# A feed-forward's closing products spread over the next unit, and a chunk's two down groups interleaved behind its last unit, with TensorE in program order

## The chip, the core and the metric

The kernel runs on one core of a Trainium2 chip. The metric is the time of one execution on the device in microseconds; several runs are made, and their median is given. The core has a matrix engine (TensorE, PE), a vector engine (VectorE, DVE), a scalar engine (ScalarE, ACT), a general engine (GpSimd, POOL) and an engine that here issues transfers (SyncE, SP). Each engine works through its own list of instructions in order, and an instruction waits for the ones on other engines that it depends on.

## The reference

One step of a decoder layer for 544 tokens (512 of a prompt and 8 requests with 4 tokens each), width 1024, hidden width 2816, in float32:

```python
def swiglu(x, wg, wu, wd):
    return (jax.nn.silu(x @ wg) * (x @ wu)) @ wd

x = layer_norm(ALPHA * x + 0.5 * swiglu(x, ffn1_wg, ffn1_wu, ffn1_wd), ln1_g, ln1_b)
...
x = layer_norm(ALPHA * x + mix, ln2_g, ln2_b)
x = layer_norm(ALPHA * x + 0.5 * swiglu(x, ffn2_wg, ffn2_wu, ffn2_wd), ln3_g, ln3_b)
```

The line left out is the mixing (RWKV-7 heads and a gated short convolution). The change touches only the two feed-forward parts, which are built by the same code. The first one fills the time from about 12 to 345 us, the second from about 700 to 1075 us.

## The kernel before, in words

Tokens lie along the columns, features along the 128 partitions. A float32 product is made of three matmuls in a reduced format: each operand x is split into a high part (an ACT copy) and a low part (DVE subtracts the high part from x), and high x high, high x low and low x high are summed in PSUM. For weights the two halves of a split are L147 (ACT) and L148 (DVE), 1024 columns at a time, into one of a few tiles hl; raw weights arrive in a few tiles raw. For activations they are L151 and L152.

The 22 hidden tiles are worked in chunks of 4, 4, 4, 4 and 6 (chunk 0 to chunk 4). For each chunk its hidden activations are computed from x, and, but for the last chunk, sent through the down weights at once and added to z, the running sum. Both steps use a Strassen-Winograd scheme: a 2 x 2 block product with seven instead of eight block products, for which sums of blocks are made first on DVE and the results are combined on DVE and ACT.

* A **unit** (pairs) is such a scheme for two hidden tiles and either the gate or the up half (even u: gate, with Silu; odd u: up, multiplied in). A product is 12 matmuls of 272 columns. The weights of a unit are split as four parts: x and a as loaded, b (the second half of x), and y, for which DVE adds blocks in two instructions first (L486, L487) and then the split follows. The products of a unit are, in their order: a at 0, a at HK, y at HK, x at HK, x at 0 (below "x0"), b, y. The last two, the **tail**, are written behind the first two products of the next unit. Where a result of PSUM bank b1 is used twice, ACT copies it out in between (L581, L587, L590 into cpb) and the next product adds on in the bank. So product x0 must wait for L587, and product b for L590. The tail's results are combined by L545 to L567 into the rows hk and sv, and put_h (L341 to L350, then L151 and L152) makes the blocks B11, NT1, B21, NT2, T3, T4 and, by put_b22, B22, that the down step multiplies.
* A **down group** (g = 0, 1) does the same for four of the eight output tiles. Its seven steps are p1, p3, p4, p5, p6, p2, p7, each with two half products (q = 0, 1) of 6 matmuls. p1 needs B11, p3 NT1, p4 B21, p5 NT2 and the weights y, p6 T3, p2 T4 and the weights b, p7 B22. DVE adds p1, p4 and p2 to z (L610), ACT copies p5 and p6 out (L626, L629), DVE subtracts p3 (L630) and adds p7 (L636), and POOL issues a DMA that accumulates the copies to the second half of z (L637): z<-cpb for group 0, z<-sv for group 1. The rows sv and the columns of cpb are written again by the next chunk's units, which so wait for these DMAs.
* Chunk 0's hidden tiles come from the plain products of up (L365, L369), and the **last chunk** has no down groups: its activations are split into hhl, and down (L390) sends them through the weights d by d.

When a weight part is split is set by a table that plan makes: for each unit or group with its start t, counted in products, part p is put at t - LEAD[p] (x 7, a 9, y 5, b 18 and other values), and feed, called at each product, issues what is due, loads too. A held instruction (hold) keeps a split from being ordered ahead of it on its engine. The order of the rest is set by a scheduler, which may slide PE's matmuls past each other as long as PSUM and data allow: pinned is False here, so the loops below say only roughly in which order PE works.

## Time and profile before

| | us |
|---|---|
| runs: median (lowest, highest) | 1082.21 (1079.39, 1083.17) |
| the profiled execution, its own time | 1080.19 |
| its span, first to last instruction | 1078.4 |
| PE busy, 8960 matmuls | 1054.3 (98%) |
| DVE busy, 1528 instructions | 833.0 (77%) |
| ACT busy, 1015 instructions | 564.3 (52%) |
| POOL busy | 206.4 (19%) |
| granted PE clock, as a share of full speed | 0.991 |

Busy shares are averages over the whole span. Where an engine works in order, what counts is which wait ends last at a place: a row of the timeline gives an instruction's start, its length, and in brackets how long its engine stood idle before it and on what. PE's matmuls overlap at their ends, so that their pace is read from start to start. The difference between a run's time and its span, 1.8 us here, lies around the first and the last instruction.

### The profile page before, as it was taken

Reading aid. Unit: us, or ns where it says so; the run is one execution under the profiler, and the core shown is the slowest. Engines: PE = TensorE matmul, PEld = TensorE weight load, DVE = VectorE, ACT = ScalarE, POOL = GpSimd, SP = SyncE. Lnnn points to the kernel's source line nnn. Section 1 sums busy time; section 2 is a strip of 40 time slices with the busy share of each in tenths; the row PEclk is TensorE's granted clock in tenths of the full one; section 3 lists DMA queues with packets and bytes.
Section 4 is the critical chain, followed back from the end, with each engine's and each line's share of the span. In section 5 each row is a group of like instructions: output and inputs, shape, how many; then the busy total and the mean of one; then the engine's idle time right before and its main releaser. Section 6 shows DMA issues by size and latency. Waiting matters only on the chain.

```text
span 1078.4 us, 22059 instructions
## 1 busy us (share of the span) xinstructions
PE 1054.3 (98%) x8960; PEld 1021.0 (95%) x8960; DVE 833.0 (77%) x1528; ACT 564.3 (52%) x1015; POOL 206.4 (19%) x296
## 2 busy tenths in 40 slices
PE   9999999999999999999999999999999999999996
PEld 8999999999999998888989899999999999999995
DVE  7798888889775857787588578878889888887755
ACT  6655565555552567555312464466554655545524
POOL 0122230312200023343220410010313122130000
PEclk9999999999999999999989999999999999999998
DMA  8568595866854231222616631424957759496302
GB/s 295 129 125 191 124 216 134 177 158 145 197 122 147 77 116 40 69 52 87 153 59 200 237 104 40 138 59 89 213 145 164 178 125 225 105 211 138 104 1 84
DMA packets 82887, 144.78 MB, mean 134 GB/s; under 512 B 20448, under 2 KB 44384, under 8 KB 82528
## 3 DMA queue, kind: packets, MB, share of 16 engines
q1 hardware_dynamic: 55584, 107.19, 30.7%
q0 software_dynamic: 27200, 36.18, 21.7%
q8 instruction: 70, 1.15, 0.4%
q14 instruction: 33, 0.27, 0.1%
HBM read 124.37 MB, written 10.06 MB: 125 GB/s over the span
## 4 chain that ended last, share of the span: by engine, by line
PE 79%; DVE 9%; DMA 6%; ACT 3%; issue 2%; SPq 0%; POOL 0%; ACTq 0%; DVEq 0%; POOLq 0%
PE mm L76 50%; PE sm L76 29%; DVE hl L148 2%; DMA z<-sv 2%; DMA z<-cpb 1%; ACT hl L147 1%; DVE De L1008 1%; DMA raw<-in_gu 1%; DVE SC L955 1%; DVE tm L1006 1%; DVE hhl L152 1%; DMA raw<-in_wd 1%; DMA DM<-Dd 1%; DMA z<-in_xT 0%; DVE z L610 0%
## 5 line engine op out<-in xcount | busy, mean ns | idle before, releaser
L76 PE MATMUL mm<-xhl,hl 128*128 128x288 f32 (+2 forms) x2640 | 362.8, 293 | 3.5 <-DVE hl L148 2.3
L76 PEld LDWEIGHTS mm<-xhl,hl 128*128 128x128 f32 x2640 | 343.6, 189 | 11.2 <-DVE hl L148 2.5
L148 DVE TENSOR_TENSOR hl<-raw,hl 128x1024 fp32r<-128x1024 f32 (+3 forms) x224 | 262.0, 1175 | 69.1 <-ACT hl L147 68.3
L147 ACT ACTIVATE hl<-raw 128x1024 fp32r<-128x1024 f32 (+3 forms) x224 | 224.4, 1012 | 91.6 <-DVE raw L487 31.3
L76 PE MATMUL sm<-xhl,hl 128*128 128x272 f32 (+1 forms) x1392 | 193.8, 289 | 0.3 <-DVE xhl L152 0.3
L76 PEld LDWEIGHTS sm<-xhl,hl 128*128 128x128 f32 x1392 | 182.3, 189 | 1.5 <-ACT xhl L151 0.6
L76 PE MATMUL mm<-tv,hl 128*128 128x272 f32 x864 | 121.3, 289 | 1.9 <-ACT cpb L587 1.8
L76 PE MATMUL mm<-hhl,hl 128*128 128x272 f32 (+2 forms) x792 | 119.2, 294 | 0.1
L76 PEld LDWEIGHTS mm<-tv,hl 128*128 128x128 f32 x864 | 113.3, 188 | 3.0 <-ACT cpb L587 2.3
L76 PEld LDWEIGHTS mm<-hhl,hl 128*128 128x128 f32 x792 | 105.9, 188 | 5.1 <-ACT sv L626 1.5
L76 PE MATMUL sm<-hhl,hl 128*128 128x272 f32 (+2 forms) x792 | 109.6, 288 | 0.0
L76 PEld LDWEIGHTS sm<-hhl,hl 128*128 128x128 f32 x792 | 103.0, 188 | 0.5
L493 POOL DMA_DIRECT2D raw<-in_gu x36 | 43.5, 1209 | 256.2 <-DVE cpb L583 81.4
L499 POOL DMA_DIRECT2D raw<-in_wd x32 | 39.3, 1469 | 269.2 <-DVE hlb L152 235.6
L76 PE MATMUL mm<-tv,hlb 128*128 128x272 f32 x432 | 61.1, 291 | 0.8 <-ACT cpb L590 0.8
L76 PEld LDWEIGHTS mm<-tv,hlb 128*128 128x128 f32 x432 | 56.4, 188 | 2.3 <-ACT cpb L590 2.2
L151 ACT ACTIVATE hhl<-sv 128x272 fp32r<-128x272 f32 (+1 forms) x52 | 26.0, 512 | 30.8 <-DVE sv L350 12.1
L152 DVE TENSOR_TENSOR hlb<-raw,hlb 128x512 fp32r<-128x512 f32 x52 | 35.7, 687 | 4.2 <-ACT hlb L151 4.2
L151 ACT ACTIVATE hhl<-hk 128x272 fp32r<-128x272 f32 (+1 forms) x48 | 24.2, 504 | 27.5 <-DVE hk L557 12.9
L218 ACT ACTIVATE lnq<-z 128x512 f32<-128x512 f32 (+1 forms) x24 | 14.9, 654 | 41.5 <-DVE z L217 41.5
L487 DVE TENSOR_TENSOR raw<-raw 128x512 f32<-128x512 f32 x52 | 35.8, 689 | 1.0
L76 PE MATMUL mm<-hhl,hlb 128*128 128x272 f32 (+2 forms) x264 | 36.4, 288 | 0.0
(294 smaller groups left out, 1325.9 us busy)
## 6 DMA issues: line engine op xcount, KB each, us to landing
raw<-in_gu SPq DMA_DIRECT2D x84, 512.0 KB, 4.6
raw<-in_gu POOLq DMA_DIRECT2D x36, 512.0 KB, 6.2
raw<-in_wd SPq DMA_DIRECT2D x32, 512.0 KB, 4.7
raw<-in_win SPq DMA_DIRECT2D x26, 512.0 KB, 3.6
raw<-in_wd POOLq DMA_DIRECT2D x32, 256.0 KB, 6.0
raw<-in_wd SPq DMA_DIRECT2D x16, 384.0 KB, 3.1
z<-cpb POOLq DMA_DIRECT2D x16, 272.0 KB, 9.0
z<-sv POOLq DMA_DIRECT2D x16, 272.0 KB, 7.3
```

The costliest lines, as they stand in the source:

```text
L76: ins = f(*args, **kw)
L147: ACT.activation(hl[:, 0, a:b], raw[:, a:b], AF.Copy)
L148: DVE.tensor_tensor(hl[:, 1, a:b], raw[:, a:b], hl[:, 0, a:b].bitcast(F32), op=OP.subtract)
L151: ACT.activation(hi, x, AF.Copy)
L152: DVE.tensor_tensor(lo, x, hi.bitcast(F32), op=OP.subtract)
L218: sq = ACT.activation(qq, zz, AF.Square)
L487: DVE.tensor_tensor(y[:, :, 0], y[:, :, 1], a[:, :, 1], op=OP.add)
L493: POOL.dma_start(x.rearrange("p (s c) -> p s c", s=2), bass.AP(tensor=a11.tensor, offset=a11.offset, ap=[[2 * D, P], [P * 2 * D, 2], [1, 5 ...
L499: POOL.dma_start(four(x)[:, i], bass.AP(tensor=a11.tensor, offset=a11.offset, ap=[[DFF, P], [P * DFF, 2], [1, 256]]), accum_op=OP.add)
L955: DVE.tensor_tensor(SC[:, p, par, a0c:a0c + n, :], q[:, :P * n].rearrange("p (c t) -> p c t", c=n), (msk if n > 1 else msks)[:, None, :].t ...
L1006: DVE.tensor_tensor(tv, AT[:, k, k + 1:32, None].to_broadcast([P, n, k + 1]), De[:, k, None, 0:k + 1].to_broadcast([P, n, k + 1]), op=OP.mult)
L1008: DVE.tensor_tensor(De[:, k + 1:32, 0:k + 1], De[:, k + 1:32, 0:k + 1], tv, op=OP.add)
```

## The change

* The tail is split in two. Product b of a unit still stands behind the next unit's two a products, but product y and what follows it now stands two products later, between x at HK and x0. For this the copy behind x0 (L590, now L602) gets columns of cpb of its own, and odd and even units use other columns.
* The chunk's last unit keeps its tail for downs, which now runs both groups in one sequence: p1 of group 0, the unit's b and y, p3(0), p1(1), p4(0), then the blocks T4 and B22 are made, p5(0), p5(1), p6(0), p3(1), p2(0), p6(1), p7(0), p2(1), p4(1). The last step, p7 of group 1, is handed to the next chunk, which does it behind its first product.
* The table of put times changes with it: group 0 of chunks 1 to 3 is counted from t - 2, group 1 from t + 4, with its y no earlier than t + 2.
* PE is kept in program order from chunk 0's down groups to the last chunk's last unit.

```diff
@@ plan
+                    add((ci, "u", u), t, dict(LEAD, b=LEAD_B.get(u, LEAD["b"] if u == 2 else 15)))
+                    t += 7
+                if ci < LAST:
+                    add((ci, "d", 0), t - 2 if ci else t, LEAD)
+                    add((ci, "d", 1), t + 4, LEAD, y=t + 2)
+                    t += 28
@@ pairs
-            def tail(u, b1, b3, cp):
+            def tail_b(u, b1, b3, cp, c2):
...
+            def tail_y(u, b1, b3, cp, c2):
...
                     if ci < LAST:
-                        self.put_h(j, 0, ("hi", "t4") if j else ("hi",))
-                        if j:
-                            self.put_b22()
+                        self.put_h(j, 0, ("hi",))
...
-                a = 0 if u % 2 else 3 * TB
-                cp = cpb[:, a:a + 3 * TB]
+                a = 0 if u % 2 else 4 * TB
+                cp, c2 = cpb[:, a:a + 2 * TB], cpb[:, (2 if u % 2 else 3) * TB:][:, :TB]
...
                 hold(ACT.activation(cp[:, 0:TB], b1, AF.Copy))
+                if u == 0:
+                    yield from self.tails.pop(0)
                 yield from prod(b4, u, "a", HK, xb(HK, 0), True)
                 hold(DVE.tensor_tensor(cp[:, 0:TB], cp[:, 0:TB], b4, op=OP.add))
-                if old is not None:
-                    yield from old
+                if u:
+                    yield from self.tails.pop(0)
                 yield from prod(b1, u, "y", HK, tb(0), False)
                 hold(ACT.activation(cp[:, TB:2 * TB], b1, AF.Copy))
                 yield from prod(b3, u, "x", HK, xb(0, TB), True)
+                if u:
+                    yield from self.tails.pop(0)
                 yield from prod(b1, u, "x", 0, tb(1), False)
-                hold(ACT.activation(cp[:, 2 * TB:], b1, AF.Copy),
-                     DVE.tensor_tensor(cp[:, 2 * TB:], cp[:, 2 * TB:], b3, op=OP.add))
-                old = tail(u, b1, b3, cp)
-            yield from old
+                hold(ACT.activation(c2, b1, AF.Copy), DVE.tensor_tensor(c2, c2, b3, op=OP.add))
+                self.tails = [tail_b(u, b1, b3, cp, c2), tail_y(u, b1, b3, cp, c2)]
@@ downs
+            yield from step["p1"](0)
+            for x in tails:
+                yield from x
+            yield from step["p3"](0)
+            b1 += [s1(), s0()]
+            yield from step["p1"](1)
+            yield from step["p4"](0)
+            if ci:
+                self.put_h(1, 0, ("t4",))
+                self.put_b22()
+            for p, g in (("p5", 0), ("p5", 1), ("p6", 0)):
+                yield from step[p](g)
+            b3 += [s0(), s0()]
+            for p, g in (("p3", 1), ("p2", 0), ("p6", 1), ("p7", 0), ("p2", 1)):
+                yield from step[p](g)
+            b4 += [s1(), s1()]
+            yield from step["p4"](1)
+            self.rest = step["p7"](1)
@@ main
+            pinned[0] = True
             for ci in range(LAST + 1):
                 if ci:
-                    yield from self.pairs(ci)
+                    yield from self.pairs(ci, self.rest)
                 if ci < LAST:
-                    yield from self.downs(ci)
+                    yield from self.downs(ci, self.tails if ci else [])
+            for x in self.tails:
+                yield from x
+            pinned[0] = False
```

The changed file has other line numbers: L486, L487 become L492, L493; L545, L547, L548 L551, L553, L554; L555 and L557 L561 and L563; L563, L565, L567 L573, L575, L577; L581, L587 L589, L597; L590 and L591 both L602; L610 L618; L626 L639; L629, L630 L628, L629; L636, L637 L632, L633. L76 to L390 are the same.

PE at the first full boundary (chunk 1), with buffer numbers. mm_1283 is b1 of chunk 1's last unit before, mm_1291 after; hlb is a part b; tv and xhl are the unit's inputs, hhl the blocks for the down groups. The rows before run from the product x0 to the first matmul of p5 of group 0:

```order
L76 MATMUL mm_1283<-tv_284,hl_1197 128x272 x12
L76 MATMUL mm_1448<-hhl_88,hl_1286 128x272 x4
L76 MATMUL mm_1283<-tv_284,hlb_1060 128x272 x12
L76 MATMUL sm_1285<-xhl_68,hl_1235 128x272 x12
L76 MATMUL mm_1448<-hhl_88,hl_1286 128x272 x2
L76 MATMUL mm_1449<-hhl_88,hl_1286 128x272 x6
L76 MATMUL sm_1450<-hhl_88,hl_1316 128x272 x6
L76 MATMUL sm_1451<-hhl_88,hl_1316 128x272 x6
L76 MATMUL sm_1452<-hhl_88,hl_1286 128x272 x6
L76 MATMUL sm_1453<-hhl_88,hl_1286 128x272 x6
L76 MATMUL mm_1448<-hhl_88,hl_1346 128x272
L76 MATMUL mm_1577<-hhl_88,hl_1491 128x272 x2
```

and after, from product b to p5 of both groups (its hl_1469 is group 1's part y):

```order
L76 MATMUL mm_1291<-tv_284,hlb_1060 128x272 x12
L76 MATMUL sm_1293<-xhl_68,hl_1236 128x272 x12
L76 MATMUL sm_1409<-hhl_88,hl_1294 128x272 x6
L76 MATMUL sm_1410<-hhl_88,hl_1294 128x272 x6
L76 MATMUL mm_1494<-hhl_88,hl_1359 128x272 x6
L76 MATMUL sm_1495<-hhl_88,hl_1359 128x272 x6
L76 MATMUL sm_1407<-hhl_88,hl_1257 128x272 x6
L76 MATMUL sm_1408<-hhl_88,hl_1257 128x272 x6
L76 MATMUL mm_1405<-hhl_88,hl_1324 128x272 x6
L76 MATMUL mm_1406<-hhl_88,hl_1324 128x272 x6
L76 MATMUL mm_1494<-hhl_88,hl_1469 128x272 x6
L76 MATMUL sm_1495<-hhl_88,hl_1469 128x272 x6
```

Before, four matmuls of p1 stood between x0 and b, and group 1 (mm_1577, with hl_1491) came in by single pairs of matmuls behind p4; after, all of p1 stands there, p1 of group 1 (mm_1494, hl_1359) goes ahead of p4, and p5 of group 1 stands right behind that of group 0.

DVE at the same place, around the two additions for part y of group 1's weights. Before:

```order
L148 TENSOR_TENSOR hl_1508<-raw_1115,hl_1508 128x1024
L630 TENSOR_TENSOR cpb_71<-cpb_71,sm_1450 128x272
L486 TENSOR_TENSOR raw_1115<-raw_1115,raw_1240 128x2x256
L630 TENSOR_TENSOR cpb_71<-cpb_71,sm_1451 128x272
L487 TENSOR_TENSOR raw_1115<-raw_1115,raw_1240 128x2x256
L610 TENSOR_TENSOR z_77<-z_77,mm_1448 128x272
L610 TENSOR_TENSOR z_77<-z_77,mm_1449 128x272
L152 TENSOR_TENSOR hlb_1557<-raw_1353,hlb_1557 128x512
L148 TENSOR_TENSOR hl_1526<-raw_1115,hl_1526 128x1024
```

and after:

```order
L346 SCALAR_TENSOR_TENSOR hk_89<-hk_89,sv_90 128x272
L347 TENSOR_TENSOR hk_89<-sv_90,hk_89 128x272
L492 TENSOR_TENSOR raw_1119<-raw_1119,raw_1241 128x2x256
L152 TENSOR_TENSOR hhl_88<-sv_90,hhl_88 128x272
L152 TENSOR_TENSOR hhl_88<-hk_89,hhl_88 128x2x272
L493 TENSOR_TENSOR raw_1119<-raw_1119,raw_1241 128x2x256
L152 TENSOR_TENSOR hlb_1484<-raw_1243,hlb_1484 128x512
L618 TENSOR_TENSOR z_77<-z_77,mm_1494 128x272
L618 TENSOR_TENSOR z_77<-z_77,sm_1495 128x272
L148 TENSOR_TENSOR hl_1469<-raw_1119,hl_1469 128x1024
```

Before, L486 and L487 stood among the steps of group 0's p6; after, L492 and L493 stand between the instructions that make NT2, T3 and T4 (L346, L347 and L152 on hhl), ahead of p1's additions for group 1.

ACT at the same place, around the copy that product b waits for. Before (L590):

```order
L587 ACTIVATE cpb_71<-mm_1283 128x272
L151 ACTIVATE hlb_1368<-raw_1115 128x512
L147 ACTIVATE hl_1346<-raw_1000 128x1024
L151 ACTIVATE hhl_88<-sv_90 128x272
L590 ACTIVATE cpb_71<-mm_1283 128x272
L151 ACTIVATE hlb_1474<-raw_1242 128x512
```

and after (L602), the same six places:

```order
L597 ACTIVATE cpb_71<-mm_1291 128x272
L147 ACTIVATE hl_1359<-raw_1241 128x1024
L575 ACTIVATE sv_90<-cpb_71 128x544
L147 ACTIVATE hl_1388<-raw_1119 128x1024
L602 ACTIVATE cpb_71<-mm_1291 128x272
L151 ACTIVATE hhl_88<-sv_90 128x272
```

Before, one split of 1024 columns (L147, hl_1346) and two short ones stood between L587's place and L590; after, two splits of group 1's weights (hl_1359 and hl_1388) and L575 stand ahead of L602.

More of the change, by code (lines that the diff above doesn't have):

```diff
@@ L446, in plan, with add @@
             items, t, events = [], 0, []
+            def add(key, at, lead, **least):
+                items.append(key)
+                events.extend((max(at - lead[part], least.get(part, -99)), key, part) for part in LEAD)
             for ci, (m0, m1) in enumerate(CHUNKS):
[L448 to L453 removed]
+                for u in range(m1 - m0 if ci else 0):
+                    add((ci, "u", u), t, dict(LEAD, b=LEAD_B.get(u, LEAD["b"] if u == 2 else 15)))
[4 more added lines that the diff above has]
+                    t += 28
             events.sort(key=lambda e: e[0])
@@ L524, in prod, with pairs @@
                     yield 6 * (TB / 2.4 + 3)
-        def pairs(self, ci):
+        def pairs(self, ci, before):
             m0, m1 = CHUNKS[ci]
@@ L544, in tail @@
                 if i == 0:
-                    hold(ACT.activation(s[:, 1, hi], cp[:, 2 * TB:], AF.Silu, scale=-1.0))
+                    hold(ACT.activation(s[:, 1, hi], c2, AF.Silu, scale=-1.0))
                 else:
-                    DVE.scalar_tensor_tensor(s[:, 1, hi], cp[:, 2 * TB:], -1.0, s[:, 1, hi], op0=OP.mult, op1=OP.mult)
+                    DVE.scalar_tensor_tensor(s[:, 1, hi], c2, -1.0, s[:, 1, hi], op0=OP.mult, op1=OP.mult)
                     hold(DVE.tensor_tensor(s[:, 0, lo], s[:, 0, lo], cp[:, 0:TB], op=OP.mult))
@@ L561, in tail @@
                         split(self.hhl[:, 0, 2 * j + 1], self.hhl[:, 1, 2 * j + 1], s[:, 1])
+            def tail_y(u, b1, b3, cp, c2):
+                j, i = divmod(u, 2)
+                s = self.rows[0] if ci < LAST and j == 0 else sv
                 yield from prod(b3, u, "y", 0, xb(HK, TB), False)
@@ new lines, in downs, with add, prods @@
+            cp = [c.rearrange("p (r t) -> p r t", r=2) for c in cps]
+            s0, s1 = (lambda: sm()[:, :TB]), (lambda: big()[:, :TB])
+            b1, b4, b3 = [s1(), s1()], [s0(), s0()], [s0(), s0()]
+            def add(d, o, op=OP.add):
+                hold(DVE.tensor_tensor(z[:, d, lo], z[:, d, lo], o, op=op))
+            def prods(g, dst, part, s, v, first, use):
+                for q in range(2):
+                    off = 2 * q if part == "b" else 4 * q + 2 * s
+                    yield from self.prod(dst[2 * g + q], (ci, "d", g), part, off, blk(v), first, 2)
+                    i, d = 2 * g + q, 4 * g + 2 * q
+                    use(i, d, dst[i])
@@ new lines, in neg, with last @@
+            def neg(i, d, o):
+                hold(ACT.activation(cp[i][:, 1], o, AF.Copy, scale=-1.0),
+                     DVE.tensor_tensor(cp[i][:, 1], cp[i][:, 1], b3[i], op=OP.subtract))
+            def last(i, d, o):
+                hold(DVE.tensor_tensor(cp[i][:, 0], cp[i][:, 0], o, op=OP.add))
+                POOL.dma_start(z[:, d:d + 2, TB:], cp[i], accum_op=OP.add)
+            step = dict(
+                p1=lambda g: prods(g, b1, "a", 0, B11, True, lambda i, d, o: add(d, o)),
+                p3=lambda g: prods(g, b3, "x", 1, NT1, True, lambda i, d, o: None),
+                p4=lambda g: prods(g, b4, "a", 1, B21, True, lambda i, d, o: add(d, o)),
+                p5=lambda g: prods(g, b1, "y", 1, NT2, False, lambda i, d, o: hold(ACT.activation(cp[i][:, 0], o, AF.Copy))),
+                p6=lambda g: prods(g, b1, "x", 0, T3, False, neg),
+                p2=lambda g: prods(g, b1, "b", 0, T4, False, lambda i, d, o: add(d + 1, o, OP.subtract)),
+                p7=lambda g: prods(g, b3, "y", 0, B22, False, last))
```

41 lines of the change are left out of this document (2 added, 39 removed).

## Prediction

> **What bounds the kernel now.** I read the page first. TensorE (PE) is busy nearly all of the span, so the kernel is its matmuls, whose number the change keeps, plus the gaps between them.
>
> ```profile
> PE 1054.3 (98%) x8960; PEld 1021.0 (95%) x8960; DVE 833.0 (77%) x1528; ACT 564.3 (52%) x1015; POOL 206.4 (19%) x296
> ```
>
> Next the waits of PE and of its weight loads (PEld), as engine, line waited for, total us, times, longest. These rows belong to the feed-forward parts:
>
> ```profile
> PE mm L76 <- ACT cpb L587: 1.8, 2, 1.4
> PE mm L76 <- ACT cpb L590: 0.8, 1, 0.8
> PEld mm L76 <- ACT cpb L590: 2.2, 7, 1.0
> PEld mm L76 <- ACT sv L626: 1.5, 8, 0.2
> PEld mm L76 <- DVE hhl L152: 1.3, 6, 0.2
> PEld mm L76 <- ACT cpb L581: 0.5, 2, 0.3
> ```
>
> Six or eight of each: they sit at the chunk boundaries, where a chunk's last unit meets its down groups (three full boundaries and one behind chunk 0 in each feed-forward part). The windows around the first full boundary and over units alone show it:
>
> ```profile
> 117.00:145.00 28.00, 27.99 (x218) 27.27 (x217) 25.27 (x49) 15.11 (x26) 6.67 (x6) 1.00 0.78 158
> 145.00:181.00 36.00, 36.00 (x288) 35.97 (x287) 29.41 (x47) 19.98 (x35) 7.40 (x7) 1.00 0.71 172
> ```
>
> Inside units 288 matmuls take 36.00 us, 125 ns each, without a gap. At the boundary DVE is busy 25.27 of 28 us (90%) and ACT 15.11, so DVE is the engine that can be late. PE's own rows there, and two behind chunk 0:
>
> ```profile
> 115.96 0.67 PE L76 MATMUL mm<-hhl,hl 128*128 128x272 f32 x4
> 116.61 1.77 PE L76 MATMUL mm<-tv,hlb 128*128 128x272 f32 x12
> 118.22 1.67 PE L76 MATMUL sm<-xhl,hl 128*128 128x272 f32 x12
> ...
> 123.73 3.01 PE L76 MATMUL mm<-hhl,hl 128*128 128x272 f32 x20
> 126.61 0.39 PE L76 MATMUL sm<-hhl,hl 128*128 128x272 f32 x1
> 126.90 1.03 PE L76 MATMUL mm<-hhl,hl 128*128 128x272 f32 x6
> 127.76 1.67 PE L76 MATMUL mm<-hhl,hlb 128*128 128x272 f32 x12
> ```
> ```profile
> 61.80 1.64 PE L76 MATMUL mm<-hhl,hl 128*128 128x272 f32 x10
> 63.27 1.67 PE L76 MATMUL mm<-hhl,hlb 128*128 128x272 f32 x12
> ```
>
> Start to start less 125 ns a matmul is the stall: 0.15 before product b, 0.11 in it (the first matmul after a stall takes about 0.1 longer), 0.38, 0.16 and 0.11 around p5: 0.9. The L626 waits of the second group (up to 0.2 each, with the restart 0.1) bring about 0.3: **1.2 us a boundary**. Behind chunk 0 the first group shows 0.22, the second about 0.3: 0.55. All of this is 6 x 1.2 + 2 x 0.55 = 8.3 us; with the last chunk's stalls below, some 12 us of 1080 is the most the change could win.
>
> **Prices.** Start-to-start times of back-to-back work:
>
> ```profile
> 117.07 0.44 DVE L547 SCALAR_TENSOR_TENSOR sv<-cpb,sv 128x272 f32<-128x272 f32 x1
> 117.54 0.44 DVE L346 SCALAR_TENSOR_TENSOR hk<-hk,sv 128x272 f32<-128x272 f32 x1
> ...
> 123.50 0.72 DVE L152 TENSOR_TENSOR hhl<-hk,hhl 128x544 fp32r<-128x544 f32 x1
> 124.14 0.43 DVE L152 TENSOR_TENSOR hhl<-sv,hhl 128x272 fp32r<-128x272 f32 x1
> 124.49 0.43 DVE L610 TENSOR_TENSOR z<-z,mm 128x272 f32<-128x272 f32 x1
> ...
> 125.79 1.22 DVE L148 TENSOR_TENSOR hl<-raw,hl 128x1024 fp32r<-128x1024 f32 x1
> 126.93 0.43 DVE L610 TENSOR_TENSOR z<-z,sm 128x272 f32<-128x272 f32 x1
> ...
> 128.76 0.69 DVE L486 TENSOR_TENSOR raw<-raw 128x512 f32<-128x512 f32 x1
> 129.36 0.43 DVE L630 TENSOR_TENSOR cpb<-cpb,sm 128x272 f32<-128x272 f32 x1
> ```
> ```profile
> 116.16 0.40 ACT L590 ACTIVATE cpb<-mm 128x272 f32<-128x272 f32 x1 [0.84 <-PE mm L76]
> 125.50 1.06 ACT L147 ACTIVATE hl<-raw 128x1024 fp32r<-128x1024 f32 x1
> 126.45 0.39 ACT L626 ACTIVATE cpb<-mm 128x272 f32<-128x272 f32 x1
> 130.43 2.01 ACT L147 ACTIVATE hl<-raw 128x1024 fp32r<-128x1024 f32 x2 [1.55 <-DVE raw L487]
> ```
>
> So DVE takes 0.35 us for 272 columns (0.47 when the next one needs its result), 0.64 for 544, 0.60 for 512, 1.14 for 1024; ACT 0.95 for a 1024 split. Product x0 ended at 115.96 and L590 began at 116.16: 0.20 from PE to its reader.
>
> The Trainium skill ("VectorE: DVE Perf Modes", section "The DRAIN you can't avoid") says that a DVE operation starts only when the one before has left the pipe. The rows disagree where operations are independent: 0.43 long, 0.35 apart. By that rule each would cost its whole length; what this would do is the last rival below.
>
> **The full boundary, walked through after's order.** Let 0 be the start of the last unit's x0, each product 1.51 us: p1(0) at 1.51, b 3.02, y 4.5, p3(0) 6.0, p1(1) 7.5, p4(0) 9.0, p5(0) 10.55, p5(1) 12.06.
>
> *Product b.* On ACT the copy that frees b's bank (L602) now stands behind a weight split that itself waits for x0's end (1.51 + 0.20): split from 1.7, L602 from 2.67 to 3.07, b due at 3.02. With the restart 0.2, and PE has no other matmuls to slip in, as it had four at 115.96.
>
> *p5(1), the heart of it.* Before, the second group's y weights were needed half a boundary after the first's. Now p5(1) follows p5(0), and y's two DVE additions (L492, L493) stand at the end of 23 DVE instructions that begin 0.2 after y(2)'s end: 17 of 272, two each of 544, 512 and 1024: 5.95 + 1.28 + 1.20 + 2.28 = 10.7 us, plus 0.4 for dependent pairs and 0.75 waiting for the first split from ACT: 0.2 + 11.85 = 12.05. Then ACT's split, 12.1 to 13.2, and DVE's low half (L148), behind a 512 and two 272, 13.35 to 14.6. PE wants the high half at 12.06 plus what it is late by then (0.8): 0.4 more; and the low half at its third matmul, 13.6: 1.0, restart 0.1.
>
> *p5(0).* The low half of its activations (L152 with 544 columns, just before L493) ends at 11.5; wanted at about 11.0: 0.5, restart 0.1.
>
> Sum 0.2 + 0.6 + 0.4 + 1.1 = 2.3 against 1.2: **+1.1 a boundary, +6.6 in six**. The bounds: 1.2 (no change), if DVE enters the boundary a microsecond ahead; 2.9, if each of the first three waits lies in front of the next.
>
> *Chunk 0.*
>
> ```profile
> 55.45 0.45 DVE L369 TENSOR_TENSOR sv<-sv,mm 128x288 f32<-128x288 f32 x1 [0.17 <-PE mm L76]
> ```
>
> This row stands 0.3 after p1(0)'s start. After, a group-1 split (1.14, less about 0.3 of idle time) goes ahead of it: it ends at 1.5 from that start. Until L493 is done come seven of 272 columns, two of 544 and three of 512, 5.5, with dependents 5.8: 7.3. ACT's split ends at 8.3, the low half at 9.5; p5(1) is due at 5 x 1.51 = 7.55, its third matmul at 8.6 by then: 0.75 + 0.9 + 0.1 = 1.75 against 0.55, **+1.2, twice: +2.4** (bounds 0 and 1.6 each).
>
> *Costs nothing:* y moved behind xHK inside units: what waits for it, L573 and L575, has a product more before their columns are reused, and cpb columns are now doubled. POOL's and SP's queues keep their order; only the last two accumulating DMAs of a chunk go a product later, behind unit 0's first product, and are wanted in the next chunk's units.
>
> *Next chunk's unit 0.* Its copy waited for z<-cpb (the L581 row); with other columns that goes: **-0.5**.
>
> *The last chunk.*
>
> ```profile
> 283.51 0.43 ACT L545 ACTIVATE sv<-cpb 128x272 f32<-128x272 f32 x1 [2.45 <-DMA z<-sv]
> 286.53 0.66 ACT L565 ACTIVATE sv<-cpb 128x544 f32<-128x544 f32 x1 [1.35 <-DVE cpb L563]
> 287.53 1.78 PE L76 MATMUL mm<-tv,hl 128*128 128x272 f32 x12 [0.41 <-ACT cpb L587]
> 976.23 1.78 PE L76 MATMUL mm<-tv,hl 128*128 128x272 f32 x12 [1.42 <-ACT cpb L587]
> 1020.57 0.63 ACT L147 ACTIVATE hlb<-raw 128x512 fp32r<-128x512 f32 x1 [2.43 <-DMA raw<-in_wd]
> 1021.10 0.38 ACT L590 ACTIVATE cpb<-mm 128x272 f32<-128x272 f32 x1
> 1021.53 1.78 PE L76 MATMUL mm<-tv,hlb 128*128 128x272 f32 x12 [0.75 <-ACT cpb L590]
> ```
>
> At its start ACT waits for z<-sv, then its copy L587 stood behind L565, which waited 1.35 for y. After, L597 stands ahead of that, and is wanted a product (1.5) later; z<-sv also goes a product later. The 1.35 and L565's half microsecond are won: all of the first stall (0.67), some 0.6 of the second: **-1.3** (bounds 0 and -2.3). At the second part's end a split that waits for a weight load stands ahead of L602 still; PE loses the four matmuls that covered 0.5, and L597 ahead of two splits delays that load 0.3: **+0.9** (bounds 0, 1.4).
>
> Sum: 6.6 + 2.4 - 0.5 - 1.3 + 0.9 = **+8.1**. The profiled execution took 1080.19 us (span 1078.4), so 1088.3. Its runs were 1079.39 to 1083.17, median 1082.21; that the profiled one lies 2.0 under the median stays in the range.
>
> **Rivals.**
> *DVE keeps ahead (faster).* If DVE works off the first third of the boundary while y(2) still runs, L493 ends 1.6 us earlier, by 10.5, and every y half is there in time; that is the point where it turns. For it: in the boundary window DVE still has 2.7 us of idle time. Against: those come later, and the 23 instructions cannot start before y(2) and L573. A boundary then costs 0.3 (restarts): -0.9 x 6 - 0.25 x 2 - 0.5 - 1.3 + 0.9 = -6.8, 1073.4; half of it 1077.
> *The waits only change places.* y arrives a microsecond earlier than walked, and p5(1) waits as long as the three old places did: 1.2 again; the rest cancels: 1080, within 0.3%.
> *A fixed PE order waits inside units.* Each of the 18 + 18 units loses 0.3 where the scheduler slipped matmuls in: +11 more, 1099. Against it: no unit shows a gap now, and their order is nearly the old one.
> *DVE operations don't overlap.* 23 x 0.08 = 1.8 us more ahead of L493 at eight places: +14, 1102; the 0.35 spacings speak against it. This is what the rule of the Trainium skill named above would give.
>
> **How the numbers follow.** A measurement of this kernel can tell about 0.3% (3 us) from no change. Chances: forecast 0.45, DVE ahead 0.30, places changed 0.18, units 0.05, no overlap 0.02. So faster 0.30, same 0.18, slower 0.52. The forecast's own range is 1083 to 1093: boundaries at +0.3 each below, at their upper bounds (+1.7, chunk 0 +1.6) above. The whole range, 1075 to 1093, reaches half into the faster case and leaves out its lower part (0.12) and the last two (0.07).
>
> **What would show it.** Right: PE idle under two names at every boundary, the waits of p5(1)'s weights (DVE hl L148, ACT hl L147) near 1.4 together and DVE hhl L152 near 0.5; the boundary's DVE idle gone; L587's stall at 287 gone. Wrong: no wait of mm<-hhl on L148 at all, PE at 224 matmuls in 28 us across a boundary, or gaps inside units.

## The result, and the profile after

| | before | after |
|---|---|---|
| median of 4 runs (lowest, highest), us | 1082.69 (1079.39, 1085.60) | 1100.81 (1096.23, 1102.31) |
| the profiled execution, us | 1080.19 | 1102.26 |
| its span, us | 1078.4 | 1100.5 |
| granted PE clock | 0.991 | 0.989 |

The changed kernel is slower: 1.0158 times the time before, 95% interval 1.0119 to 1.0196. The forecast was 1088.3 with a range up to 1093: the direction holds, the size doesn't.

The page's first part for after, which answers the row that opened the prediction:

```profile
PE 1058.8 (96%) x8960; PEld 1021.2 (93%) x8960; DVE 827.5 (75%) x1528; ACT 557.1 (51%) x1015; POOL 205.9 (19%) x296
```

The same 8960 matmuls, and a span 22.1 us longer: the loss is gaps between matmuls. Its waits of PE (engine, line waited for, total us, times, longest):

```profile
PE mm L76 <- DVE hl L148: 8.4, 9, 2.3
PE mm L76 <- ACT cpb L597: 4.4, 4, 1.7
...
PE mm L76 <- ACT cpb L602: 2.4, 3, 1.1
...
PE mm L76 <- ACT hl L147: 1.9, 2, 1.5
PE mm L76 <- ACT cpb L589: 1.5, 4, 0.5
...
PE mm L76 <- DVE hhl L152: 0.7, 4, 0.2
```

There are two families. L148, L147 and L152 on hhl are the halves of p5's operands, as forecast (one 2.3 of L148 lies elsewhere in the kernel and stood there before). L597, L602 and L589 are copies out of PSUM that a unit's next product waits for. All four of L589 and 1.3 of L597 lie in units where the forecast had no new wait; the two longest of L597 (1.73 and 1.31) and one of L602 (1.08) lie at the last chunk's start. The other two of L602 stand before a product b, one at the sixth boundary (0.78) and one at the second part's end (0.51).

A wait's row names only what it saw. So I also added up, from PE's rows, every step from one matmul's start to the next that is longer than 156 ns, less the usual 126 ns, by the place where it lies. In us, both feed-forward parts together, one execution of each kernel (single executions of before lie up to 6.2 us apart, so a difference of 1 or 2 us between two kernels' sums says little):

| | chunk 0 | 6 boundaries | units | last start | last end | sum |
|---|---|---|---|---|---|---|
| before | 1.1 | 7.1 | 0.8 | 2.5 | 1.8 | 13.2 |
| after | 6.7 | 15.1 | 6.0 | 4.9 | 1.6 | 34.3 |
| change | +5.6 | +8.0 | +5.2 | +2.5 | -0.2 | +21.1 |
| forecast | +2.4 | +6.6 | -0.5 | -1.3 | +0.9 | +8.1 |

These places hold 21.1 of the 22.1 us.

**The boundary.** After's first full boundary, PE (with one row of its weight loads, PEld), DVE and ACT:

```profile
118.79 1.78 PE L76 MATMUL mm<-tv,hlb 128*128 128x272 f32 x12
...
126.94 2.27 PE L76 MATMUL mm<-hhl,hl 128*128 128x272 f32 x13 [0.17 <-DVE hhl L152]
129.97 0.77 PE L76 MATMUL mm<-hhl,hl 128*128 128x272 f32 x4 [0.77 <-DVE hl L148]
...
141.94 1.17 PEld L76 LDWEIGHTS mm<-xhl,hl 128*128 128x128 f32 x9 [0.21 <-DVE z L618]
```
```profile
126.80 0.69 DVE L493 TENSOR_TENSOR raw<-raw 128x512 f32<-128x512 f32 x1
127.40 0.68 DVE L152 TENSOR_TENSOR hlb<-raw,hlb 128x512 fp32r<-128x512 f32 x1
...
128.70 1.22 DVE L148 TENSOR_TENSOR hl<-raw,hl 128x1024 fp32r<-128x1024 f32 x1
```
```profile
127.58 1.06 ACT L147 ACTIVATE hl<-raw 128x1024 fp32r<-128x1024 f32 x1 [1.59 <-DVE raw L493]
```

Read the three together: L493 makes y and is done at 127.40 (its successor's start), ACT's split of it follows at 127.58, DVE's low half at 128.70, and PE goes on at 129.97, as soon as that is done. The stalls, start to start with the restart: product b 0.25, p5(0) 0.44, p5(1)'s high half 0.39, its low half 1.03, and 0.26 at 141.94, where the next unit waits for z (L618): 2.4. And DVE has nothing left to give in the first 13 us of it. It was nearly as full before; what is new is that PE wants its results sooner. The rows of before, then after (columns: PE, PEld, DVE, ACT, POOL):

```profile
117.00:130.00 13.00, 12.99 (x101) 12.56 (x100) 12.65 (x28) 6.88 (x14) 1.82 (x2) 1.00 0.54 98
117.00:130.00 13.00, 11.94 (x90) 11.04 (x88) 12.97 (x27) 6.82 (x13) 1.21 (x1) 1.00 0.24 68
```

**The units.** One of the new gaps, in the next chunk's first unit:

```profile
154.10 1.67 PE L76 MATMUL mm<-tv,hlb 128*128 128x272 f32 x12
154.86 1.06 ACT L147 ACTIVATE hl<-raw 128x1024 fp32r<-128x1024 f32 x1 [2.97 <-DMA raw<-in_gu]
155.82 0.38 ACT L589 ACTIVATE cpb<-mm 128x272 f32<-128x272 f32 x1
156.25 1.78 PE L76 MATMUL mm<-tv,hl 128*128 128x272 f32 x12 [0.48 <-ACT cpb L589]
```

PE names the copy L589, but the copy itself is short. It stands in ACT's list behind a weight split that waited 2.97 us for a load, and that is the cause one step further back. What POOL issues around there, before and then after:

```profile
133.53 2.44 POOL L637 DMA_DIRECT2D z<-cpb  x2 [0.28 <-DVE cpb L636]
141.37 1.21 POOL L493 DMA_DIRECT2D raw<-in_gu  x1 [5.39 <-DVE z L610]
146.01 2.43 POOL L637 DMA_DIRECT2D z<-sv  x2 [3.43 <-DVE sv L636]
```
```profile
140.41 1.21 POOL L633 DMA_DIRECT2D z<-cpb  x1 [5.62 <-DVE cpb L632]
141.90 1.21 POOL L633 DMA_DIRECT2D z<-cpb  x1 [0.28 <-DVE z L618]
144.40 1.21 POOL L499 DMA_DIRECT2D raw<-in_gu  x1 [1.30 <-DVE z L618]
147.72 1.20 POOL L633 DMA_DIRECT2D z<-sv  x1 [2.11 <-DVE sv L632]
149.20 1.20 POOL L633 DMA_DIRECT2D z<-sv  x1 [0.28 <-DVE cpb L593]
```

The accumulating z<-cpb went from 133.5 to 140.4 and 141.9, right ahead of the loads for the next unit. The load at 141.37 took 6.5 us to land before; the one at 144.40 takes 10.2 (DMA issues of those microseconds, before and after):

```profile
raw<-in_gu POOLq DMA_DIRECT2D x1, 512.0 KB, 6.5
```
```profile
raw<-in_gu POOLq DMA_DIRECT2D x1, 512.0 KB, 10.2
```

At the last chunk's start it is z<-sv itself that is late. ACT's and PE's rows there:

```profile
295.00 0.43 ACT L551 ACTIVATE sv<-cpb 128x272 f32<-128x272 f32 x1 [5.94 <-DMA z<-sv]
297.00 1.77 PE L76 MATMUL mm<-tv,hl 128*128 128x272 f32 x12 [1.73 <-ACT cpb L597]
```

ACT waited 2.45 us for it before and 5.94 now, with the copy L597 behind.

### The profile page after: what moved, and what is told of

Same layout as the page of the kernel before. It is cut to its first block, busy times and chain, and to the rows that moved or that the text cites. A ratio compares the mean times of both kernels' runs of the same rounds, so it can differ in the third digit from the quotient of the medians.

```text
span 1100.5 us, 22097 instructions
## 1 busy us (share of the span) xinstructions
PE 1058.8 (96%) x8960; PEld 1021.2 (93%) x8960; DVE 827.5 (75%) x1528; ACT 557.1 (51%) x1015; POOL 205.9 (19%) x296
## 4 chain that ended last, share of the span: by engine, by line
PE 57%; DVE 20%; DMA 10%; ACT 7%; issue 5%; POOL 0%; SPq 0%; ACTq 0%; DVEq 0%; POOLq 0%
PE mm L76 37%; PE sm L76 19%; DMA raw<-in_wd 6%; DVE hl L148 6%; ACT hl L147 3%; DMA z<-sv 2%; DVE hhl L152 2%; DVE raw L493 1%; DVE z L618 1%; DVE raw L492 1%; DVE hlb L152 1%; DMA raw<-in_gu 1%; DVE SC L982 1%; DVE De L1035 1%; DVE tm L1033 1%
## 5 line engine op out<-in xcount | busy, mean ns | idle before, releaser
L76 PE MATMUL mm<-xhl,hl 128*128 128x288 f32 (+2 forms) x2640 | 364.0, 295 | 3.6 <-DVE hl L148 2.3
L76 PEld LDWEIGHTS mm<-xhl,hl 128*128 128x128 f32 x2640 | 344.5, 190 | 12.8 <-DVE hl L148 2.5
L148 DVE TENSOR_TENSOR hl<-raw,hl 128x1024 fp32r<-128x1024 f32 (+3 forms) x224 | 262.1, 1175 | 79.8 <-ACT hl L147 78.8
L147 ACT ACTIVATE hl<-raw 128x1024 fp32r<-128x1024 f32 (+3 forms) x224 | 226.2, 1014 | 159.6 <-DVE raw L493 78.0
L76 PE MATMUL sm<-xhl,hl 128*128 128x272 f32 (+1 forms) x1392 | 189.2, 289 | 0.4 <-DVE xhl L152 0.3
L76 PEld LDWEIGHTS sm<-xhl,hl 128*128 128x128 f32 x1392 | 179.8, 189 | 2.1 <-DVE xhl L152 1.0
L76 PE MATMUL mm<-tv,hl 128*128 128x272 f32 x864 | 121.9, 290 | 6.1 <-ACT cpb L597 4.4
L76 PE MATMUL mm<-hhl,hl 128*128 128x272 f32 (+2 forms) x744 | 112.8, 295 | 9.5 <-DVE hl L148 6.1
L76 PEld LDWEIGHTS mm<-tv,hl 128*128 128x128 f32 x864 | 113.2, 188 | 8.7 <-ACT cpb L597 6.1
L76 PE MATMUL sm<-hhl,hl 128*128 128x272 f32 (+2 forms) x840 | 116.1, 289 | 0.0
L76 PEld LDWEIGHTS mm<-hhl,hl 128*128 128x128 f32 x744 | 100.0, 190 | 15.5 <-DVE hl L148 7.8
L76 PEld LDWEIGHTS sm<-hhl,hl 128*128 128x128 f32 x840 | 109.8, 189 | 0.0
L76 PE MATMUL mm<-tv,hlb 128*128 128x272 f32 x432 | 61.3, 292 | 2.4 <-ACT cpb L602 2.4
L76 PEld LDWEIGHTS mm<-tv,hlb 128*128 128x128 f32 x432 | 56.4, 188 | 4.4 <-ACT cpb L602 4.3
L152 DVE TENSOR_TENSOR hlb<-raw,hlb 128x512 fp32r<-128x512 f32 x52 | 35.8, 688 | 25.5 <-ACT hlb L151 25.4
L151 ACT ACTIVATE hlb<-raw 128x512 fp32r<-128x512 f32 x52 | 32.6, 627 | 30.1 <-DMA raw<-in_wd 27.7
L151 ACT ACTIVATE hhl<-sv 128x272 fp32r<-128x272 f32 (+1 forms) x52 | 25.9, 512 | 34.8 <-DVE sv L350 12.2
L151 ACT ACTIVATE hhl<-hk 128x272 fp32r<-128x272 f32 (+1 forms) x48 | 24.1, 503 | 26.5 <-DVE hk L347 16.0
L618 DVE TENSOR_TENSOR z<-z,mm 128x272 f32<-128x272 f32 x64 | 27.0, 433 | 13.2 <-PE mm L76 13.2
L493 DVE TENSOR_TENSOR raw<-raw 128x512 f32<-128x512 f32 x52 | 35.8, 688 | 0.9
```

Source lines behind the costliest of these rows:

```text
L76: ins = f(*args, **kw)
L147: ACT.activation(hl[:, 0, a:b], raw[:, a:b], AF.Copy)
L148: DVE.tensor_tensor(hl[:, 1, a:b], raw[:, a:b], hl[:, 0, a:b].bitcast(F32), op=OP.subtract)
L151: ACT.activation(hi, x, AF.Copy)
L152: DVE.tensor_tensor(lo, x, hi.bitcast(F32), op=OP.subtract)
L493: DVE.tensor_tensor(y[:, :, 0], y[:, :, 1], a[:, :, 1], op=OP.add)
```

## The experiments

Theories. **A**: at the boundaries and behind chunk 0 the y halves come late from a full DVE, as walked in the prediction. **B**: in the units and at the last chunk's start, the accumulating transfers, now late, fall together with the next chunk's loads. **C**, against B: the loads and splits are late there without the transfers, through the new order and table alone. **D**: the fixed PE order is what costs. All ratios are against before, run on the same chip, with 95% intervals.

### The boundary

e1_p5late puts p5(1) two steps later:

```diff
-            for p, g in (("p5", 0), ("p5", 1), ("p6", 0)):
+            for p, g in (("p5", 0), ("p6", 0)):
...
-            for p, g in (("p3", 1), ("p2", 0), ("p6", 1), ("p7", 0), ("p2", 1)):
+            for p, g in (("p3", 1), ("p5", 1), ("p2", 0), ("p6", 1), ("p7", 0), ("p2", 1)):
```

> The changed kernel with one step moved: p5 of group 1 stands behind p6(0) and p3(1) instead of right behind p5(0). Theory A (the late y half): the waits of p5(1) for the split of group 1's y weights, 1.3 us at each of the six full boundaries and 1.6 and 2.7 us behind the two chunks 0, go; 12 us less, about 1089 against 1100.8. Rival (DVE is full at the boundary, whatever waits there): the wait moves to another step of the same boundary, and the time stays at 1100 within 2 us. Stalls inside units stay as they are under both.

Measured 1092.72 us, 1.0091 (1.0073 to 1.0108). Of PE's waits the new one:

```profile
PE mm L76 <- ACT cpb L639: 3.1, 7, 0.7
```

The y waits are gone (the L148 row is down to the 2.3 that stood before), chunk 0 falls from 6.7 to 2.9 and the boundaries from 15.1 to 10.7. They don't fall to 7.1, because p6(0) now follows p5(0) directly and waits for the copy L639. A holds; some of it changes places.

e12_yearly makes y earlier instead:

```diff
-                    add((ci, "d", 1), t + 4, LEAD, y=t + 2)
+                    add((ci, "d", 1), t + 4, LEAD)
```

> The changed kernel without the lower bound t + 2 on group 1's part y, whose two additions and split then stand 13 DVE instructions earlier, ahead of the blocks NT2, T3 and T4. Theory A: the waits of p5(1) for y (1.3 us a boundary, 1.6 and 2.7 behind chunk 0) go, but DVE's 2.3 us of y work now stand ahead of p5(0)'s block, whose wait of 0.4 grows to about 2: boundaries as now, chunk 0 better by 3 us in all, 1097. Rival (the y half was late for another reason, its weights or buffers): p5(1) still waits, 1101 or more.

Measured 1106.02, 1.0219 (1.0193 to 1.0245), worse than after. PE's and DVE's rows at the first boundary:

```profile
125.87 1.01 PE L76 MATMUL mm<-hhl,hl 128*128 128x272 f32 x6 [1.90 <-DVE sv L563]
```
```profile
121.52 0.68 DVE L493 TENSOR_TENSOR raw<-raw 128x512 f32<-128x512 f32 x1
...
123.60 1.23 DVE L148 TENSOR_TENSOR hl<-raw,hl 128x1024 fp32r<-128x1024 f32 x1
...
125.38 0.43 DVE L563 SCALAR_TENSOR_TENSOR sv<-mm,sv 128x272 f32<-128x272 f32 x1
```

y is ready 5 us sooner, and product b's combination L563, at 122.00 in after, now stands behind it at 125.38. It frees the bank that p1(1) needs, so PE stops there; the boundaries bring 24.1 us (6.1 of them matmuls at half the clock behind four of these stalls, see the last section), and only chunk 0 gains (3.7 instead of 6.7). DVE is full: what is moved ahead makes something else late.

e7_nopin takes away the fixed order:

```diff
-            pinned[0] = True
```

> The changed kernel with PE's order left to the scheduler instead of program order. Rival D (a fixed order loses the matmuls that the scheduler slid into the gaps): boundary stalls fall from 2.4 to about 1.4, those in units halve, 1090. Theories A and B (what is wanted is late, whoever orders PE): at most a microsecond or two in all, 1099.

Measured 1089.16, 1.0076 (1.0054 to 1.0098). The boundaries come down to 8.4 and chunk 0 to 1.2, near before's, while the units' gaps stay and even grow (9.0 instead of 6.0). PE at p5(1):

```profile
127.61 0.68 PE L76 MATMUL mm<-hhl,hl 128*128 128x272 f32 x3 [0.23 <-ACT hl L147]
128.13 0.41 PE L76 MATMUL sm<-hhl,hl 128*128 128x272 f32 x2
128.38 1.53 PE L76 MATMUL mm<-hhl,hl 128*128 128x272 f32 x11
```

The two matmuls at 128.13 belong to another step and bridge the time until the low half is there. Is the fixed order then dear by itself? e10_before_pin gives it to the kernel before:

```diff
+            pinned[0] = True
             for ci in range(LAST + 1):
...
+            pinned[0] = False
```

> The kernel before, with nothing changed but PE in program order from the first down groups to the last chunk's last unit. Theory D (a fixed order by itself exposes the waits that the scheduler covered): boundaries rise from 3.5 us a part to 6 or more, 1087. Theory A (only the interleaved order asks for y's halves too soon): boundaries stay, 1082.

Measured 1083.88, 1.0016 (1.0000 to 1.0033): at most 3.6 us. In its one profile the boundaries do rise, from 7.1 to 10.7, through 0.75 before each product b, where the scheduler had four matmuls to slip in; after, with all of p1 there, pays 0.25 at five of the six. So D alone is not it: the interleaved steps ask for the halves too early, and the fixed order takes away the cover that would have hidden it.

### The units and the last chunk's start

e3_nodma is after without the accumulating transfers, and e4_before_nodma the same of before:

```diff
-                POOL.dma_start(z[:, d:d + 2, TB:], cp[i], accum_op=OP.add)
```
```diff
-                    POOL.dma_start(z[:, ds[q]:ds[q] + 2, TB:], cp[q], accum_op=OP.add)
```

> The changed kernel without the accumulating transfers z<-cpb and z<-sv; it leaves out a part of the down products in the second half of the tokens. Theory B (those transfers crowd the weight loads, which land late in front of the copies of a unit): the stalls inside units (6 us) and at the last chunk's start (5 us) go: 1090. Rival C (the loads are late because their buffers come free later on DVE): loads are issued as late as now, only the last chunk's start is won, 1096.

> The kernel before without the accumulating transfers, as a control; it leaves out the same part of the down products. Its waits for them are 0.7 and 1.7 us at the last chunk's start and 0.4 us at a unit: 3 us less, 1080. If contention costs the kernel before as much as the one after, 6 us more than that.

e3 took 1092.12, 1.0088 (1.0057 to 1.0119; two runs); e4 1077.87, 0.9961 (0.9946 to 0.9975). In e3 the units fall from 6.0 to 1.8 and the last chunk's start from 4.9 to nothing; the boundaries stay (14.4). The place of the unit's gap above, in e3:

```profile
154.03 1.68 PE L76 MATMUL mm<-tv,hlb 128*128 128x272 f32 x12
155.55 1.68 PE L76 MATMUL mm<-tv,hl 128*128 128x272 f32 x12
```

12 matmuls in 1.52 us, no gap. The load that was issued at 144.40 in after is issued at 144.33 here, so not its time of issue but what is under way beside it has changed. A load on SP's queue, issued at 143.50 in after and 143.44 here, lands after 6.2 and 3.7 us, so the transfers delay loads of the other queue too. The load on POOL's queue still takes long to land:

```profile
raw<-in_gu POOLq DMA_DIRECT2D x1, 512.0 KB, 9.2
```

Only 1.0 of the 3.7 us that it takes longer than before is the transfers' doing; the rest comes without them. Landing 1.0 sooner is just enough for the copy L589 to be in time. So B decides the stall here, and C is part of why there is so little to spare. What makes the rest is not shown: in e3 three loads are issued within 2.4 us (143.44, 144.33, 145.83), in before the same three within 3.7 (140.47, 141.37, 144.19), and no run spreads them again.

By the measured times the transfers cost 0.70% after and 0.39% before. The intervals are too wide to tell these two apart. The stalls of the profiles put the difference at 7.7 us: 34.3 falls to 24.4 in e3, 13.2 to 11.0 in e4.

e13_before_late_cpb tests B from the other side: the kernel before, with the two z<-cpb held back behind the second group's p6. A column of DVE work that adds 0 times p6's result holds them, and cpb has after's columns. Its control e14_before_layout has only those columns:

```diff
-                a = 0 if u % 2 else 3 * TB
-                cp = cpb[:, a:a + 3 * TB]
+                a = 0 if u % 2 else 4 * TB
+                cp, c2 = cpb[:, a:a + 2 * TB], cpb[:, (2 if u % 2 else 3) * TB:][:, :TB]
```

and e13 further:

```diff
+                    if g:
+                        dst, src = late.pop(0)
+                        DVE.scalar_tensor_tensor(src[:, 0, 0:1], b1[q][:, 0:1], 0.0, src[:, 0, 0:1], op0=OP.mult, op1=OP.add)
+                        POOL.dma_start(dst, src, accum_op=OP.add)
...
-                    POOL.dma_start(z[:, ds[q]:ds[q] + 2, TB:], cp[q], accum_op=OP.add)
+                    late.append((z[:, ds[q]:ds[q] + 2, TB:], cp[q]))
+                    if g:
+                        POOL.dma_start(*late.pop(), accum_op=OP.add)
```

> As the experiment before it was meant: the kernel before with cpb's columns laid out as in the changed kernel, and group 0's z<-cpb made to leave behind group 1's p6 by a one-column operation on DVE that adds 0 times p6's result (two such operations a chunk). Theory B: z<-cpb leaves some 6 us later, beside the next chunk's weight loads, which land 3 to 5 us later than now; units and the last chunk's starts lose 3 to 6 us, 1085. Rival C: loads and units as before, 1080.

> The kernel before with the changed layout of cpb's columns alone (a copy of x0 in columns of its own, even and odd units apart from the ones of z<-cpb), as a control for the experiment above and as a version that may beat both. The wait of the copy L581 for z<-cpb (0.5 us) goes and nothing else changes: 1080 to 1081.5 where before is 1082, too little to tell surely.

e13 took 1086.99, 1.0050 (1.0032 to 1.0069), e14 1080.01, 0.9980 (0.9965 to 0.9995): with before's own order of products, transfers that are issued later cost 0.7%. In e13 the z<-cpb went at 140.23 and 141.84 (133.91 in e14), one z<-sv also moved, to 143.30 from 146.31, and the load between them landed as follows, in e13 and then in e14:

```profile
raw<-in_gu POOLq DMA_DIRECT2D x1, 512.0 KB, 11.9
```
```profile
raw<-in_gu POOLq DMA_DIRECT2D x1, 512.0 KB, 7.4
```

In e13's first unit ACT waits for it as in after, and PE behind ACT:

```profile
154.42 1.06 ACT L147 ACTIVATE hl<-raw 128x1024 fp32r<-128x1024 f32 x1 [3.16 <-DMA raw<-in_gu]
```
```profile
160.21 1.77 PE L76 MATMUL mm<-tv,hl 128*128 128x272 f32 x12 [1.10 <-ACT cpb L587]
```

That is B without any of the interleaving. But e13's units bring only 1.8 us, against 1.0 in e14. Most of its loss stands at the last chunk's start (8.4 against 3.5), in one stall of the second part, where z<-sv itself is late; ACT's row in e13:

```profile
979.96 0.43 ACT L545 ACTIVATE sv<-cpb 128x272 f32<-128x272 f32 x1 [5.86 <-DMA z<-sv]
```

This wait was 3.68 us in e14. The two z<-sv landed there after 11.4 and 12.2 us, against 6.2 and 9.1, and PE then stood still for 4.50 behind the copy L587. So late transfers delay each other as well as the loads.

An earlier try of this experiment, e11_before_crowd, had the same edit without the DVE column:

> The kernel before, with group 0's two transfers z<-cpb issued behind group 1's p6 instead of behind their own p7, some 6 us later, just ahead of z<-sv, as in the changed kernel; cpb's columns are laid out as there, so that no unit waits for them. Theory B (crowded transfers make the next chunk's weight loads late): stalls in units and at the last chunk's start rise from 3.3 us to 7 or more, 1086. Rival C (loads are late for their buffers): as before, 1081.

It took 1079.42, 0.9981 (0.9964 to 0.9998), but its z<-cpb were still issued at 133.88, since nothing held the scheduler to the written place. It says nothing on B and agrees with e14.

e2_p7now takes p7(1) back from the next chunk:

```diff
-            self.rest = step["p7"](1)
+            yield from step["p7"](1)
+            self.rest = ()
```

> The changed kernel with p7 of group 1 at the end of its own chunk instead of behind the next chunk's first product. Theory B (transfers land late): z<-sv is issued one product (1.5 us) earlier, the last chunk's start waits 1.5 us less in each part (3.3 and 1.6 us now), 3 us in all: 1098. Rival (the late z<-sv comes from the order on DVE, not from p7's place): no change, 1101.

Measured 1100.50, 1.0167 (1.0144 to 1.0189): nothing won (its boundaries bring 13.1 us instead of 15.1, its units 10.7 instead of 6.0). DVE before the last chunk:

```profile
281.30 2.35 DVE L148 TENSOR_TENSOR hl<-raw,hl 128x1024 fp32r<-128x1024 f32 x2
283.57 0.78 DVE L632 TENSOR_TENSOR sv<-sv,sm 128x272 f32<-128x272 f32 x2
```

The subtraction L632 that z<-sv waits for is queued behind two splits for the next unit, so that z<-sv is issued at 284.36 and 285.10, no sooner than in after (282.69 and 284.17). Counted from the first z<-cpb of the same chunk it is 7.3 and 8.0 us, against 7.3 and 8.8. To hand p7(1) on is not what made it late.

e8_spread puts p2(0) and p7(0) ahead of p5(1), so that z<-cpb comes sooner:

```diff
-            for p, g in (("p5", 0), ("p5", 1), ("p6", 0)):
+            for p, g in (("p5", 0), ("p6", 0)):
...
-            for p, g in (("p3", 1), ("p2", 0), ("p6", 1), ("p7", 0), ("p2", 1)):
+            for p, g in (("p3", 1), ("p2", 0), ("p7", 0), ("p5", 1), ("p6", 1), ("p2", 1)):
```

> The changed kernel with another order of steps behind p4(0): p5(0), p6(0), p3(1), p2(0), p7(0), p5(1), p6(1), p2(1), p4(1). p5(1) is later, as in the first experiment, and p7(0) three steps earlier, so that z<-cpb leaves some 6 us earlier. Theory A: the boundary falls as there, to 1.7 us or less. Theory B: with the two pairs of transfers apart, loads land earlier, stalls in units fall by half (3 us) and at the last chunk's start by 2 us: 1087. Rival C (buffers free late): units as in the first experiment, 1092.

Measured 1092.80, 1.0115 (1.0081 to 1.0149). z<-cpb is issued early, and the units fall from 6.0 to 3.2, the last start from 4.9 to 3.0; POOL's row:

```profile
134.93 2.45 POOL L633 DMA_DIRECT2D z<-cpb  x2 [0.18 <-issue]
```

B's part of this is there, the number isn't B's: the boundaries stay at 14.7 with waits for L639 as in e1. And the load behind, issued at 142.96, still takes 9.7 us: the z<-cpb have landed by 143.66, but the two z<-sv are issued beside it, at 146.27 and 147.76.

### The two halves of the change alone

e5_tailonly gives the kernel before only the split tail, y behind x at HK of the next unit; e6_downsonly is after with y put back behind b there:

```diff
-                if old is not None:
-                    yield from old
+                if old:
+                    yield from old.pop(0)
...
+                if old:
+                    yield from old.pop(0)
```
```diff
                 if u:
                     yield from self.tails.pop(0)
+                    yield from self.tails.pop(0)
...
-                if u:
-                    yield from self.tails.pop(0)
```

> The kernel before with one part of the change alone: a unit's closing product y moved behind x at HK of the next unit; down groups one after the other, PE's order left to the scheduler. Boundaries and transfers stay, so under theories A and B nothing is lost: 1082 within 2 us, and up to 1.5 us won at the last chunk's start where the copy no longer stands behind the Silu that waits for y. Rival (the spread itself makes units wait): the 6 us of stalls in units appear here, 1088.

> The changed kernel with y back behind b inside units: the other part of the change alone (interleaved down groups, p7 of group 1 deferred, fixed order). Theories A and B put nearly all of the loss here: 1098 to 1102. Rival (the spread makes units wait): the stalls inside units go, 1094.

e5 took 1082.90, 1.0018 (1.0001 to 1.0035); its one profile, of its slowest execution (1087.26), has stalls of 17.2, with 2.6 in units and 9.4 at boundaries. e6 took 1113.81, 1.0306 (1.0274 to 1.0338), a miss: no theory had it slower than after. PE's first wait in e6:

```profile
PE mm L76 <- ACT cpb L598: 19.0, 10, 3.3
```

With the old unit's y between x at HK and x0, the copy L597 (here L598) has a product more before x0 wants it. Without that, the units lose 21.7 us: 15.8 in stalls, and 5.9 in matmuls at half the clock behind the longest of them. In all, the halved clock costs 9.6 us in e6's stall sum and 1.5 in after's. So the spread tail is worth about 13 us to the interleaved order, by giving late loads slack and by keeping the stalls short, and nothing that can be measured to the order before, whose loads were in time.

### Both causes away

e9_nopin_spread is e7 and e8 together, e15_nopin_nodma e7 and e3 together; both consist of the lines shown.

> The changed kernel with the order of steps of the spread experiment and PE left to the scheduler. If boundaries (theories A and D: late halves that a free order covers) and crowded transfers (theory B) are separate costs, the two gains add: boundaries near 4.2 us a part as with the free order, units and last start near those of the spread order: 1084. If the free order only moves the same waits, 1089.

> The changed kernel with PE's order left to the scheduler and without the accumulating transfers (it leaves out a part of the down products in the second half of the tokens). If late halves under a fixed order and crowded transfers are all of the loss, it comes down to the kernel before without these transfers, 1078; if something else is left, 1083 or more.

e9 took 1089.82, 1.0067 (1.0044 to 1.0091): no better than e7. Its profile has the units at 1.6 but the boundaries at 11.3, so the gains don't add; why the boundaries rise again I didn't take apart. e15 took 1081.30, 1.0000 (0.9987 to 1.0014): with a free PE order and no accumulating transfers the changed kernel is as fast as before, and its stalls, 13.1, are those of before (13.2). Against e4, the fair mate, 3.4 us stay; its units and boundaries show 2.3 of them, the rest I can't place.

## Why the prediction was right and wrong

*The direction* was right, for the reason given first. *The boundary walk* was right step by step: L493 was to end 12.05 us after x0's start, and ended 11.8 after (x0's first matmul at 115.62, where its product of 12 begins); p5(1)'s low half was to run from 13.35 to 14.6 and ran from 13.1 to 14.3; the stalls came out at 0.25, 0.44, 0.39 and 1.03 against 0.2, 0.6, 0.4 and 1.1. Six boundaries brought +8.0 against +6.6; the difference is mostly the wait for z (L618) at a boundary's end, which the walk left out, and 0.8 more before product b at the sixth. e1 shows that the y halves cause it, e12 that DVE has no room to mend it, and e7 and e10 that the fixed order only lays it bare. One reading ahead of the walk was loose: "six or eight of each" holds for three of the six waits listed there, and those of PE for L587 and L590 are the last chunk's.

*Chunk 0* was right in the first part (+1.4 against +1.2) and too low in the second (+4.2). Of that, 1.7 is a clock that the walk couldn't see (below); the rest goes with L493, which ended 0.4 us after p5(1) was due there (at 762.8), where it had ended 0.75 before in the first part: two splits of 544 columns (xhl from cpb) stood later among its predecessors.

*The failed step* is the one called "Costs nothing": "only the last two accumulating DMAs of a chunk go a product later, behind unit 0's first product, and are wanted in the next chunk's units." It looked at who wants the transfers' result, not at what they share the DMA engines with, and it looked at group 1's two only. Group 0's p7 had moved as well, behind most of group 1, and with it the z<-cpb, by 6.9 us (about 2.7 of it the stalls up to there), next to the next unit's loads. The units then lose 5.2 where the forecast had -0.5. e3 (the transfers away: units at 1.8, no stall at the last chunk's start) and e13 (the transfers late: a new stall in a unit, and z<-sv late at the last chunk) show it from both sides. The same step also held that POOL's and SP's queues lose nothing while they keep their order. They keep it at the first boundary, and yet 2.7 of the 3.7 us by which the load lands later are there without the transfers; the cause of these 2.7 stays open.

*The last chunk's start*, forecast at -1.3, is the same step once more: "z<-sv also goes a product later" was written down, and then only the instructions behind y were counted as won. z<-sv goes later and takes longer, ACT waits 5.94 instead of 2.45, and the term is +2.5. *The last end*, +0.9, did not come (-0.2): 1.1 too much.

Of the rivals, DVE did not keep ahead: the point from which that decides was L493's end at 10.5, and it was 11.8. The waits did not merely change places. "A fixed PE order waits inside units", at 1099, named a place and nearly the time, but not the cause: e7 frees the order and the units' gaps stay. And 1100.8 lies close to the 1102 of the rival in which DVE operations don't overlap, but by accident: these rows of after still start 0.35 apart at a length of 0.43,

```profile
122.00 0.43 DVE L563 SCALAR_TENSOR_TENSOR sv<-mm,sv 128x272 f32<-128x272 f32 x1
122.35 0.43 DVE L573 TENSOR_TENSOR cpb<-cpb,sm 128x272 f32<-128x272 f32 x1
```

(The rule that the prediction set beside this rival, from the Trainium skill's section "The DRAIN you can't avoid" of "VectorE: DVE Perf Modes", has an exception in the same section: an operation that is not held starts earlier. So these rows do not speak against that page.) The range was too narrow because its bounds were nearly all for work on DVE, ACT and PE; none stood for transfers and loads that land later at a chunk's change, or for a halved clock.

The best version found is e14, before with after's columns of cpb: 1080.01, 0.2% under before (0.05 to 0.35%). The wait that this layout takes away was forecast at 0.5 us; its one profile doesn't show the gain (its stalls sum to 14.4).

## What to carry to other kernels

When a change moves the step that feeds a transfer, cost the transfer at its new place against the loads that are under way there, even if nobody wants its result soon. On an engine that works in order, a copy that PE wants next should not stand behind a split that waits for a load: PE's row then names the copy, and the cause is one step further back. A fixed order is cheap (0.16% here) as long as operands are early; before interleaving two sequences, check that the engine that makes the operands has idle time in just those microseconds. And a stall of PE can cost more than its length, as the next section shows.
